# One hand-divided tile for w_down's blocks and their sums, with six block places in the 6-tile products

## The chip, the cores and the metric

One core of a Trainium2 chip runs the kernel. The metric is the device time of one execution in microseconds (us), as the median of several runs.

## The reference

One layer of a hybrid decoder in float32, on 512 tokens with 16 learned meta tokens ahead of them (D = 2048, feed-forward width 5632):

```python
n = rmsnorm(h, g_mix);  p = n @ w_in            # q, k, v | b, c, u
o = concat(rmsnorm(stick_breaking_attention(q, k, v)),      # 8 heads of 128
           rmsnorm(b * causal_dwconv3(c * u)))              # 1024 channels
h = h + o @ w_out
n2 = rmsnorm(h, g_ffn)
h = h + (silu(n2 @ w_gate) * (n2 @ w_up)) @ w_down
return h[:, N_META:]
```

The change lies in the preparation of the weights of the last two lines, the feed-forward part, and in the places that `w_out`'s tiles share with them.

## The kernel before

**Products.** A float32 product is made of three products of rounded halves: each operand is split into hi (a rounded copy) and lo (the rest), and TensorE adds hi·hi, hi·lo and lo·hi (L702, L703 and L704). Weights are the stationary operand, 128x128 at a time; 256 token columns stream past.

**Pairs.** Gate, up and down are computed by a scheme that does a 2x2 block product with 7 products instead of 8. A *pair* is one such set of four weight blocks, 11, 12, 21 and 22. There are 44 pairs of gate and up (8 k tiles a block, pairs 0 to 43), four pairs of `w_down` that hold two output columns of 4 k tiles each (pairs 44 to 47, results 512 wide), and 24 pairs of `w_down` with 6 k tiles (pairs 48 to 71, in three chunks of the feed-forward width). The seven products of a pair use, in this order, the weights 11, t1 = 11+12, t2 = t1+22, 22, t3 = 12+22, 21 and t2+21. They accumulate into three PSUM banks in the order x, z, x, z, x, y, x. `pair_product` drains them: ScalarE copies x, z, x after products 1, 2 and 3 (L727, L729, L731); VectorE reads z after product 4 (L733) and x after product 5 (L737), and y after product 6 (L740). Product 7 writes bank x again, and so it cannot begin before L737 has read it.

**Preparation of weights.** It runs two products ahead of TensorE (`S_AHEAD` = 2), in steps of `prepare_pair`. `load_quad` (L591) issues the DMA of one block on SyncE's queue (SP). `split_quad` makes hi on ScalarE (L609) and lo on VectorE (L610). `add_quads` makes t1 and t3 on VectorE (L616), L650 makes t2 in t1's buffer, and `add_last` (L623) adds 21 into t2. A block of the next pair is loaded as soon as the same block of this pair has been read for the last time: 11 after t1, 12 after t3, 22 after its split, 21 after it has been added into t2. `load_wide` (L601) fetches `w_out`'s tiles into the same buffers before pair 0.

**Buffers.** Pool `sw` has one buffer for each of the tags `b11`, `b12`, `b21` and `b22`, two for the tag `sum` (t1 and t3 take them in turn), and three for the tag `s` (hi and lo of a product): 48 KB of each partition. In pairs with 6 k tiles a quarter of each buffer is unused.

**Order.** The kernel is written in product order, and a scheduler orders each engine's queue by the dependences of the tiles; the preparation has high priority. Which instruction stands first on VectorE therefore depends on which buffer comes free first.

**Other queues.** `gate` turns products into activations, splits them (L187 and L188) and stores them to DRAM by GpSimd's queue (POOL, L894), the last ones by SP's (L896); `load_acts` brings them back into a ring of places on POOL's queue (L932). `down` adds the results of the first chunks into the output in DRAM (L961, POOL).

Of the kernel before, what the change touches and what calls it, by code (L numbers as in the profile page):

```python
# [9 lines left out]
F32 = mybir.dt.float32  # L10
F32R = mybir.dt.float32r
# [4 lines left out]
P = 128  # L16
# [6 lines left out]
KT = D // P  # L23
FT = FF // P
# [9 lines left out]
def hybrid_layer(ctx: ExitStack, tc: tile.TileContext, xT, w_in, w_out, w_gu, w_down, vecs, out):  # L34
# [12 lines left out]
    def open_pool(name, bufs=1, **kw):  # L47
        return tc.alloc_tile_pool(name=name, bufs=bufs, reuse_waits="tile", **kw)
# [509 lines left out]
    sw = open_pool("sw", side="right")  # L558
    acc_h = hpool.tile([P, SEQ], F32, name="acc_h")
    hpool.tile([P, 24], F32, name="pad_h")  # L560
    pairs = []
# [17 lines left out]
    quads, sums, split_w, used = {}, {}, [], [0]  # L579
    S_AHEAD = 2  # L580
    ORDER = ("21", "11", "12", "22")
    WIDE = 2 * KT - 2

    def load_quad(i, q):
        if i < len(pairs):
            n, srcs = pairs[i]
            quads[i, q] = sw.tile([P, 8 * P], F32, tag=f"b{q}", name=f"b{q}_{i}")[:, : n * P]
            src, dst = srcs[("11", "12", "21", "22").index(q)], quads[i, q]
            if len(src.shape) == 3:
                dst = dst.rearrange("p (t c) -> p t c", t=2)  # L590
            nc.sync.dma_start(dst, src)  # L591

    wide = []

    def load_wide():

        i = len(wide)
        q = ORDER[(i + 2) % 4]
        if i < WIDE:
            wide.append(sw.tile([P, 8 * P], F32, tag=f"b{q}", name=f"wide{i}"))  # L600
            nc.sync.dma_start(wide[i], w_out[OUT_TILES[1 + i // 2], i % 2])  # L601
        else:
            wide.append(None)
            load_quad(0, q)

    def split_quad(src, n):
        t = sw.tile([P, 2, 8 * P], F32R, tag="s", bufs=S_AHEAD + 1, name=f"s{len(split_w)}")
        hi, lo = (t[:, i, : n * P] for i in range(2))
        sc.copy(hi, src)  # L609
        ve.tensor_tensor(lo, src, hi.bitcast(F32), ALU.subtract)  # L610
        split_w.append((hi, lo))

    def add_quads(i, name, a, b):
        n = pairs[i][0]
        sums[name] = sw.tile([P, 8 * P], F32, tag="sum", bufs=2, name=f"{name}_{i}")[:, : n * P]
        ve.tensor_tensor(sums[name], a, b, ALU.add)  # L616

    def add_t3(i, b):
        add_quads(i, "t3", b["12"], b["22"])
        load_quad(i + 1, "12")  # L620

    def add_last(i, b):
        ve.tensor_tensor(sums["t2"], sums["t2"], b["21"], ALU.add)  # L623
        load_quad(i + 1, "21")


    FIRST_ORDER = (5, 0, 1, 2, 3, 4, 6)
# [1 line left out]
    def prepare_pair():  # L629
        if len(split_w) < WIDE:  # L630
            with tc.high_priority():
                split_quad(wide[len(split_w)], 8)
                load_wide()
            return
        i, s = divmod(len(split_w) - WIDE, 7)
        if i == len(pairs):
            return
        n = pairs[i][0]
        if i == 0:
            s = FIRST_ORDER[s]  # L640
        with tc.high_priority():
            b = {q: quads[i, q] for q in ("11", "12", "21", "22") if (i, q) in quads}
            if s == 0:
                split_quad(b["11"], n)
                add_quads(i, "t1", b["11"], b["12"])
                load_quad(i + 1, "11")
            elif s == 1:
                split_quad(sums["t1"], n)
                sums["t2"] = sums["t1"]
                ve.tensor_tensor(sums["t2"], sums["t2"], b["22"], ALU.add)  # L650
                if i:
                    add_t3(i, b)
            elif s == 2:
                split_quad(sums["t2"], n)
                if not i:
                    add_t3(i, b)
            elif s == 3:
                split_quad(b["22"], n)
                load_quad(i + 1, "22")
            elif s == 4:  # L660
                split_quad(sums["t3"], n)
            elif s == 5:
                split_quad(b["21"], n)
                if i:
                    add_last(i, b)
            else:
                if not i:
                    add_last(i, b)
                split_quad(sums["t2"], n)

    def prepare_ahead(n):
        while len(split_w) < min(WIDE + 7 * len(pairs), used[0] + n):
            prepare_pair()
# [96 lines left out]
    for _ in range(4):  # L770
        load_wide()
# [11 lines left out]
    for i, j in enumerate(OUT_TILES):  # L783
# [8 lines left out]
        half, k = divmod(j, 8)  # L792
# [285 lines left out]
```

## Time and profile before

| what | value |
| --- | --- |
| runs | 2084.57, 2085.06 and 2085.66 us; median 2085.06 |
| profiled execution | 2083.91 us, span on the chip 2082.2 us, mean granted clock 0.998 |
| TensorE busy (PE) | 2056.2 us, 99% of the span |
| VectorE busy (DVE) | 1627.0 us, 78% |
| ScalarE busy (ACT) | 1016.3 us, 49% |
| GpSimd busy (POOL) | 370.4 us, 18% |
| weight blocks of gate and up, issue to landing | 176 loads of 512 KB, median 3.7 us |
| blocks of `w_down`, two columns | 16 loads of 512 KB, median 7.6 us |
| blocks of `w_down`, 6 k tiles | 96 loads of 384 KB, median 3.7 us |
| activations back from DRAM (ring) | 42 loads of 768 KB, median 13.3 us |

The span is the time from the first to the last instruction on the core; the execution's own time is slightly longer. Busy shares are means over stages with different limits, so what counts is what TensorE waits for in each stage. In the rows, a number in brackets behind an instruction is the idle time of its engine before it and what ended it; `t<-b,b` is a sum of two blocks, `s<-b,s` or `s<-t,s` the lo half of a split, `b<-w_down` a load.

### The profile page before, as it was taken

What the parts mean: (1) busy time and instruction counts of PE and PEld (TensorE: products, weight loads), DVE (VectorE), ACT (ScalarE), POOL (GpSimd) and SP (SyncE); (2) the same over time, 40 slices, a digit from 0 to 9 for tenths busy, and PEclk for the clock granted to TensorE, in tenths of its full rate; (3) what the DMA queues carried; (4) which work ended last, traced back from release to release, by engine and by line L of the source; (5) the groups of instructions that cost most, each with busy time, mean ns of one, the idle gap of its engine ahead of it and who ended that gap; (6) DMA issues with size and microseconds to landing.
All of it is one profiled execution on the core that took longest, in us unless ns stands there. A gap on an engine that the chain in (4) does not pass through costs nothing.

```text
span 2082.2 us, 39144 instructions
## 1 busy us (share of the span) xinstructions
PE 2056.2 (99%) x16086; PEld 1982.1 (95%) x16086; DVE 1627.0 (78%) x2133; ACT 1016.3 (49%) x1522; POOL 370.4 (18%) x499
## 2 busy tenths in 40 slices
PE   8999999999999999999999999999999999999999
PEld 7899999999998888999999999999999999989999
DVE  6877777533336769999898898898988977878888
ACT  6666666322223434555555555555555544444443
POOL 0111111010103454111111011011111242121210
PEclk9999999999999999999999999999999999999999
DMA  5222222222225557546555464455455999697764
GB/s 186 72 72 77 77 82 72 82 97 94 93 101 167 185 179 239 158 137 195 166 149 170 149 177 153 148 172 167 135 175 158 279 340 339 149 323 171 209 149 110
DMA packets 144116, 330.41 MB, mean 159 GB/s; under 512 B 12400, under 2 KB 62064, under 8 KB 143936
## 3 DMA queue, kind: packets, MB, share of 16 engines
q1 hardware_dynamic: 67456, 212.50, 30.6%
q0 software_dynamic: 76480, 115.40, 21.6%
q8 instruction: 126, 2.06, 0.4%
q14 instruction: 54, 0.44, 0.1%
HBM read 260.74 MB, written 67.11 MB: 157 GB/s over the span
## 4 chain that ended last, share of the span: by engine, by line
PE 91%; DVE 4%; DMA 3%; ACT 1%; issue 1%; SPq 0%; POOL 0%; DVEq 0%; ACTq 0%; POOLq 0%
PE x L702 10%; PE x L704 10%; PE x L703 10%; PE z L702 5%; PE z L704 5%; PE z L703 5%; PE po L682 3%; PE po L683 3%; PE po L681 3%; PE y L704 3%; PE y L703 3%; PE y L702 3%; DMA b<-w_down 2%; PE pv L173 2%; PE pv L175 2%; PE pu L177 1%
## 5 line engine op out<-in xcount | busy, mean ns | idle before, releaser
L609 ACT CAST s<-t 128x1024 fp32r<-128x1024 f32 (+1 forms) x288 | 283.2, 983 | 373.7 <-PE z L704 164.1
L610 DVE TENSOR_TENSOR s<-t,s 128x1024 fp32r<-128x1024 f32 (+1 forms) x288 | 326.8, 1135 | 99.4 <-ACT s L609 97.4
L704 PE MATMUL x<-f,s 128*128 128x256 f32 x1408 | 387.4, 275 | 1.7 <-DVE s L610 1.7
L703 PE MATMUL x<-f,s 128*128 128x256 f32 x1408 | 387.5, 275 | 0.2 <-DVE f L188 0.2
L702 PE MATMUL x<-f,s 128*128 128x256 f32 x1408 | 387.4, 275 | 0.2 <-ACT f L187 0.2
L609 ACT CAST s<-b 128x1024 fp32r<-128x1024 f32 (+1 forms) x216 | 212.4, 983 | 156.6 <-PE x L704 138.0
L704 PEld LDWEIGHTS x<-f,s 128*128 128x128 f32 x1408 | 264.3, 188 | 1.9 <-DVE s L610 1.9
L702 PEld LDWEIGHTS x<-f,s 128*128 128x128 f32 x1408 | 264.3, 188 | 0.7 <-ACT f L187 0.4
L703 PEld LDWEIGHTS x<-f,s 128*128 128x128 f32 x1408 | 264.3, 188 | 0.5 <-DVE f L188 0.4
L610 DVE TENSOR_TENSOR s<-b,s 128x1024 fp32r<-128x1024 f32 (+1 forms) x216 | 246.5, 1141 | 2.4 <-ACT s L609 1.8
L142 DVE TENSOR_TENSOR wlo<-raw,whi 128x512 fp32r<-128x512 f32 (+1 forms) x198 | 139.3, 705 | 134.8 <-ACT whi L141 133.9
L894 POOL DMA_DIRECT2D fd<-s x147 | 103.7, 922 | 690.5 <-DVE s L188 674.0
L141 ACT CAST whi<-raw 128x512 fp32r<-128x512 f32 (+1 forms) x198 | 121.1, 614 | 192.0 <-PE pu L175 65.6
L702 PE MATMUL z<-f,s 128*128 128x256 f32 x704 | 193.8, 275 | 0.7 <-ACT sides L729 0.7
L703 PE MATMUL z<-f,s 128*128 128x256 f32 x704 | 193.8, 275 | 0.2 <-DVE f L188 0.2
L704 PE MATMUL z<-f,s 128*128 128x256 f32 x704 | 193.7, 275 | 0.0
L616 DVE TENSOR_TENSOR t<-b,b 128x1024 f32<-128x1024 f32 (+1 forms) x144 | 165.5, 1149 | 21.8 <-DMA b<-w_down 17.3
L702 PE MATMUL x<-ring,s 128*128 128x256 f32 x608 | 167.8, 276 | 8.8 <-DVE d L737 6.4
L704 PE MATMUL x<-ring,s 128*128 128x256 f32 x608 | 167.4, 275 | 0.5 <-DVE s L610 0.5
L703 PE MATMUL x<-ring,s 128*128 128x256 f32 x608 | 167.3, 275 | 0.0
L702 PEld LDWEIGHTS z<-f,s 128*128 128x128 f32 x704 | 132.2, 188 | 0.9 <-ACT sides L729 0.9
L703 PEld LDWEIGHTS z<-f,s 128*128 128x128 f32 x704 | 132.2, 188 | 0.4 <-DVE f L188 0.4
(349 smaller groups left out, 5588.0 us busy)
## 6 DMA issues: line engine op xcount, KB each, us to landing
b<-w_gu SPq DMA_DIRECT2D x176, 512.0 KB, 3.7
raw<-w_in SPq DMA_DIRECT2D x92, 512.0 KB, 3.2
fd<-s POOLq DMA_DIRECT2D x147, 256.0 KB, 5.3
b<-w_down SPq DMA_DIRECT2D x96, 384.0 KB, 3.7
ring<-fd POOLq DMA_DIRECT2D x42, 768.0 KB, 13.3
wide<-w_out SPq DMA_DIRECT2D x30, 512.0 KB, 3.3
out_T<-d POOLq DMA_DIRECT2D x54, 256.0 KB, 4.7
b<-w_down SPq DMA_DIRECT2D x16, 512.0 KB, 7.6
```

Of the source, the lines that this page charges most:

```text
L141: sc.copy(hi[:, :c], raw)
L142: ve.tensor_tensor(lo[:, :c], raw, hi[:, :c].bitcast(F32), ALU.subtract)
L609: sc.copy(hi, src)
L610: ve.tensor_tensor(lo, src, hi.bitcast(F32), ALU.subtract)
L616: ve.tensor_tensor(sums[name], a, b, ALU.add)
L681: pe.matmul(ps, hi[:, kk], ah, start=k == 0, stop=False)
L682: pe.matmul(ps, hi[:, kk], al, start=False, stop=False)
L683: pe.matmul(ps, lo[:, kk], ah, start=False, stop=k == 7)
L702: pe.matmul(p, hi[:, kk], act[:, 0, k], start=start and j == k == 0, stop=False, skip_group_check=skip)
L703: pe.matmul(p, hi[:, kk], act[:, 1, k], start=False, stop=False, skip_group_check=skip)
L704: pe.matmul(p, lo[:, kk], act[:, 0, k], start=False, stop=k == n - 1, skip_group_check=skip)
L894: gp.dma_start(fd[c][s][:, :, k], t[:, :, i])
```

## The change

The pool's tags are replaced by two tiles that are divided by hand and have the same size together. `sw_split` holds the three hi and lo places in turn. `sw_in` holds blocks and sums. With 8 k tiles it has six places: four for blocks, one each for t1 (in which t2 is made) and t3. With 6 k tiles it has eight: six that the blocks take in turn, one each for t1 and t3. From pair 48 on, `load_next` gives a freed place to the block that is six blocks further on: when 11 is free, 22 of the next pair is loaded; when 12 is free, 21 of the next pair; when 22 is free, 11 of the pair after the next; when 21 is free, 12 of that pair. Before pair 48 a freed block is followed by the same block of the next pair, as it was. Line numbers behind this part move: L591 becomes L604, L609 and L610 become L632 and L633, L616 becomes L639, L733 becomes L758, L737 becomes L762.

```diff
+    QUADS = ("11", "12", "22", "21")
+    SIX = FT + KT // 4
+    sw_in = sw.tile([P, 6 * 8 * P], F32, name="sw_in")
+    sw_split = sw.tile([P, 6 * 8 * P], F32R, name="sw_split")
+
+    def w_place(t, n, i):
+        return t[:, i * n * P : (i + 1) * n * P]
+
+    def quad_place(i, q):
+        m = QUADS.index(q)
+        return w_place(sw_in, pairs[i][0], m if i < SIX else (4 * (i - SIX) + m) % 6)
+
     def load_quad(i, q):
         if i < len(pairs):
             n, srcs = pairs[i]
-            quads[i, q] = sw.tile([P, 8 * P], F32, tag=f"b{q}", name=f"b{q}_{i}")[:, : n * P]
+            quads[i, q] = quad_place(i, q)
...
+    def load_next(i, q):
+
+        m = QUADS.index(q)
+        if i < SIX:
+            load_quad(i + 1, q)
+            if i + 1 == SIX and m == 3:
+                load_quad(SIX + 1, QUADS[0])
+        else:
+            load_quad(i + 1 + (m + 2) // 4, QUADS[(m + 2) % 4])
...
-            wide.append(sw.tile([P, 8 * P], F32, tag=f"b{q}", name=f"wide{i}"))
+            wide.append(quad_place(0, q))
...
     def split_quad(src, n):
-        t = sw.tile([P, 2, 8 * P], F32R, tag="s", bufs=S_AHEAD + 1, name=f"s{len(split_w)}")
-        hi, lo = (t[:, i, : n * P] for i in range(2))
+        k = len(split_w) % (S_AHEAD + 1) * 2
+        hi, lo = (w_place(sw_split, n, k + i) for i in range(2))
...
     def add_quads(i, name, a, b):
         n = pairs[i][0]
-        sums[name] = sw.tile([P, 8 * P], F32, tag="sum", bufs=2, name=f"{name}_{i}")[:, : n * P]
+        sums[name] = w_place(sw_in, n, (4 if n == 8 else 6) + (name == "t3"))
         ve.tensor_tensor(sums[name], a, b, ALU.add)
 
     def add_t3(i, b):
         add_quads(i, "t3", b["12"], b["22"])
-        load_quad(i + 1, "12")
+        load_next(i, "12")
 
     def add_last(i, b):
         ve.tensor_tensor(sums["t2"], sums["t2"], b["21"], ALU.add)
-        load_quad(i + 1, "21")
+        load_next(i, "21")
...
-                load_quad(i + 1, "11")
+                load_next(i, "11")
...
-                load_quad(i + 1, "22")
+                load_next(i, "22")
...
                 split_quad(sums["t2"], n)
+                if i + 1 == SIX:
+                    load_quad(SIX + 1, QUADS[1])
```

## The prediction

> **What bounds the kernel now.** I read the busy time by stretches first: the gate/up pairs (833 to 1626), the four pairs of `w_down` with two output columns (1626 to 1722), and the pairs with products of 6 k tiles, where the six places are (1722 to 2060).
>
> ```profile
> core 0: us, PE busy (x) PEld busy (x) DVE busy (x) ACT busy (x) POOL busy (x), PEclk, DMA share, GB/s
> 833.00:1626.00 793.00, 792.32 (x6991) 792.12 (x6990) 714.26 (x800) 416.81 (x542) 105.11 (x149) 1.00 0.53 160
> 1626.00:1722.00 96.00, 95.41 (x840) 95.03 (x839) 79.55 (x81) 48.57 (x59) 33.05 (x40) 1.00 1.11 330
> 1722.00:2060.00 338.00, 329.21 (x2892) 328.21 (x2891) 288.17 (x386) 152.09 (x230) 63.63 (x78) 1.00 0.80 216
> ```
>
> TensorE is the bound everywhere: it misses 0.7 us of 793, 0.6 of 96, and 8.8 of 338. The change issues the same matmuls, so it can gain only from the last row's 8.8 us, and it loses wherever it makes TensorE wait. The waits of PE in 1722 to 2060 say what the 8.8 are:
>
> ```profile
> PE x L702 <- DVE d L737: 6.4, 4, 2.5
> PE x L702 <- ACT s L609: 2.4, 2, 1.5
> ```
>
> Six waits, all at the start of a pair's seventh product. That product writes the PSUM bank `x` that L737 reads, so it waits for L737. What L737 waits for stands in the chain of waits and the timeline, for the longest of the six:
>
> ```profile
> 1832.52 8.18 DMA b<-w_down
> ```
>
> ```profile
> 1840.79 0.96 DVE L616 TENSOR_TENSOR t<-b,b 128x768 f32<-128x768 f32 x1 [3.27 <-DMA b<-w_down]
> 1841.67 0.42 DVE L737 SCALAR_TENSOR_TENSOR d<-x,sides 128x256 f32<-128x256 f32 x1
> ```
>
> ```profile
> 1842.23 0.36 PE L702 MATMUL x<-ring,s 128*128 128x256 f32 x1 [2.50 <-DVE d L737]
> ```
>
> The load is block 22 of the next pair, issued when 22 of this pair has been split, 8.18 us on its way. t3 = 12+22 stands in DVE's queue for it, L737 stands behind t3, and 0.14 us after L737's end (1842.09) the product starts. So a late block 22 costs TensorE time through DVE's order, not because TensorE needs that block yet.
>
> **What the change takes away.** From pair 48 on, the load of 22 of the next pair goes out when 11 of this pair has been split, not 22.
>
> ```profile
> 1824.48 0.95 DVE L610 TENSOR_TENSOR s<-b,s 128x768 fp32r<-128x768 f32 x1
> ...
> 1833.53 0.96 DVE L616 TENSOR_TENSOR t<-b,b 128x768 f32<-128x768 f32 x1
> ```
>
> ```profile
> DMA to landing us min/median/max: 3.0/6.1/8.5
> ```
>
> The first row is the split of 11 in the pair of that stall; the load can be issued at its end, 1825.43, instead of 1832.52. The last line is the time to landing of all weight loads issued from 1820 to 1880. Even with 8.5 us it lands at 1833.9, where the sum waited until 1840.79. The 8.8 us go, all of them as far as these rows show. With each stall's restart counted I would not go over 10.
>
> **What the change adds unsaid: the order of the two sums.** Before, t1 and t3 take turns in two buffers (tag `sum`). The next pair's t1 takes the buffer that t3 has just left, the next t3 that of t2 (t2 is summed into t1's buffer, and is read last). After, t1 has a place of its own for ever and t3 another. The next t1 cannot be written until the last split of t2 has read its place; the next t3 can, as soon as t3 has been split. So in the built program DVE's order turns, in nearly every pair from the first gate/up pair on: before s(t3), t1', s(21), L733, s(t2), t3', L737; after s(t3), **t3'**, s(21), L758 (the old L733), s(t2), **t1'**, L762 (the old L737), where s() is the subtraction of a split and ' is the next pair. t1' needs blocks 11 and 12, t3' needs 12 and 22. Block 22 is therefore wanted where 11 was, four places sooner, and outside the 6-tile pairs its load is issued at the same event as before. Queued behind the waiting t3' on DVE are s(21) and s(t2), which TensorE's products 6 and 7 need, and L762, on whose bank product 7 waits. PE's order is the same; SP's, ACT's and POOL's nearly (two ring loads on POOL's queue go ahead of an output accumulation).
>
> Gate/up, an even pair:
>
> ```profile
> 1216.05 0.33 SPq L591 DMA_DIRECT2D b<-w_gu  x1
> ```
>
> ```profile
> DMA to landing us min/median/max: 3.1/3.1/3.1
> ```
>
> ```profile
> 1218.16 1.22 DVE L616 TENSOR_TENSOR t<-b,b 128x1024 f32<-128x1024 f32 x1
> ...
> 1224.32 0.42 DVE L737 SCALAR_TENSOR_TENSOR u<-x,sides 128x256 f32<-128x256 f32 x1
> ...
> 1226.01 0.28 PE L702 MATMUL x<-f,s 128*128 128x256 f32 x1
> ```
>
> Block 22 lands at 1219.15; t3' moves to where t1' starts, 1218.16: a wait of 1.0 us. L737 ends at 1224.74 and, with 0.14, has 1.13 us before the product that needs it. So it costs 0, though only just; DVE's idle time in between is a further reserve. In odd pairs the 128x1280 split of the activations goes ahead of t3', and the block is there. Only the first pair is worse: its block 22 lands late.
>
> ```profile
> 821.33 1.43 DVE L616 TENSOR_TENSOR t<-b,b 128x1024 f32<-128x1024 f32 x1 [0.98 <-DMA b<-w_gu]
> ```
>
> There t1' (1.15, below) used to run ahead of that wait and now comes behind it: +1.2.
>
> The two-column pairs, where loads are slow. Pair 45, DVE and then the start of its seventh product:
>
> ```profile
> 1674.60 1.23 DVE L610 TENSOR_TENSOR s<-t,s 128x1024 fp32r<-128x1024 f32 x1 [1.05 <-ACT s L609]
> 1675.86 1.23 DVE L616 TENSOR_TENSOR t<-b,b 128x1024 f32<-128x1024 f32 x1
> 1677.27 1.22 DVE L610 TENSOR_TENSOR s<-b,s 128x1024 fp32r<-128x1024 f32 x1 [0.18 <-ACT s L609]
> 1678.97 0.69 DVE L733 SCALAR_TENSOR_TENSOR d_first<-z,d_first 128x512 f32<-128x512 f32 x1 [0.48 <-PE z L704]
> 1679.98 1.23 DVE L610 TENSOR_TENSOR s<-t,s 128x1024 fp32r<-128x1024 f32 x1 [0.33 <-ACT s L609]
> 1681.63 1.23 DVE L616 TENSOR_TENSOR t<-b,b 128x1024 f32<-128x1024 f32 x1 [0.42 <-DMA b<-w_down]
> 1682.78 0.68 DVE L737 SCALAR_TENSOR_TENSOR d_first<-x,d_first 128x512 f32<-128x512 f32 x1
> ```
>
> ```profile
> 1684.14 0.28 PE L702 MATMUL x<-first,s 128*128 128x256 f32 x1
> ```
>
> t3' waited for its block until 1681.63. Now everything from s(21) on stands behind that. From start to next start: sum 1.15 (1681.63 to 1682.78), split 1.22 (its duration), combination 0.68 (its duration 0.69, less the overlap), split 1.26 (1674.60 to 1675.86), sum 1.15, L762 0.68, and 0.14 to PE: 6.28. The product starts at 1681.63 + 6.28 = 1687.9 instead of 1684.14: **+3.8**. The other pairs by the same chain, from when their t3' has its block to when product 7 started:
>
> ```profile
> 1642.40 1.23 DVE L616 TENSOR_TENSOR t<-b,b 128x1024 f32<-128x1024 f32 x1 [0.38 <-DMA b<-w_down]
> ...
> 1644.89 0.28 PE L702 MATMUL x<-f,s 128*128 128x256 f32 x1
> ...
> 1662.27 1.23 DVE L616 TENSOR_TENSOR t<-b,b 128x1024 f32<-128x1024 f32 x1
> ...
> 1664.19 0.36 PE L702 MATMUL x<-first,s 128*128 128x256 f32 x1
> ...
> 1700.69 1.23 DVE L616 TENSOR_TENSOR t<-b,b 128x1024 f32<-128x1024 f32 x1 [0.45 <-DMA b<-w_down]
> ...
> 1703.18 0.28 PE L702 MATMUL x<-first,s 128*128 128x256 f32 x1
> ```
>
> Pair 43, the last of gate/up, has 256-wide combinations (0.42 each, so 0.5 less): 1642.40 + 5.8 - 1644.89 = **+3.3**. Pair 46: 1700.69 + 6.28 - 1703.18 = **+3.8**. Pair 44: there s(21) goes ahead of t3' (so 5.06 behind it), and 1662.27 + 5.06 - 1664.19 = +3.1 at most. But pair 43's stall shifts that pair's loads by 3.3, and POOL's queue has run out by then:
>
> ```profile
> L932 POOL DMA_DIRECT2D first<-fd x2: 703/716/730, 1645.4 to 1646.0; - x2
> ...
> DMA to landing us min/median/max: 14.1/14.7/15.4
> ```
>
> ```profile
> DMA to landing us min/median/max: 4.6/4.6/4.6
> ```
>
> POOL's last loads of that burst land by 1661.4; the second line is the weight load issued between 1660 and 1661, in that gap. The sum of 1662.27 waited for nothing, so the block was there by then; if its load starts 3.3 later but takes 4.6 us, not the 6.6 (below) to 8.2 (above) of loads beside POOL's, it lands 2 to 3.6 sooner after its issue, which is about the shift and about the price: pair 44 **0**, with 3.1 as the other end. Pair 47, whose next pair is the first with 6 tiles:
>
> ```profile
> 1711.77 0.33 SPq L591 DMA_DIRECT2D b<-w_down  x1
> ```
>
> ```profile
> DMA to landing us min/median/max: 6.6/6.6/6.6
> ```
>
> ```profile
> 1722.22 0.28 PE L702 MATMUL x<-first,s 128*128 128x256 f32 x1
> ```
>
> Landing 1718.4, then the chain with 768-wide sums (0.88 by 1840.79 to 1841.67, twice) and one 768-wide split ahead of L762 (0.87): 6.28 - 0.54 + 0.87 = 6.6; 1718.4 + 6.6 - 1722.22 = **+2.8**, from 0 if POOL's queue has run out here too.
>
> A rule of the Trainium skill bears on these loads: its page "DMA: Bandwidth & Descriptors", section "Queues, rings and completion order", says that each DMA engine takes turns, packet by packet, between the queue rows that have work, so a weight load beside POOL's transfers gets only its turns. The trace agrees: the load of 1711.77 took 6.6 us, those in the gap and in gate/up 4.6 and 3.1. By that rule alone a pair whose load falls into a gap would cost nothing, which is rival (a).
>
> The last thing added is 221 wait-only instructions on DVE (the lo subtraction now names its wait for PE too). Such waits exist already:
>
> ```profile
> L610 DVEq EVENT_SEMAPHORE  x2: 21/21/21, 1210.3 to 1229.4; - x2
> ```
>
> At 21 ns each they could come to 4.6 us if all were on the path. DVE is idle for 79 of the 793 us of gate/up while TensorE misses 0.7, so I take 0, and keep 1 for the range.
>
> **Sum.** 1.2 + 3.3 + 0 + 3.8 + 3.8 + 2.8 = 14.9 lost, 8.8 gained: +6.1. I take 0.5 off, for the load's time in pairs 45 to 47 as the stretched stage thins the traffic: **+5.6**. The rows come from the profiled execution, 2083.9 us (span 2082.2), which would become 2089.5; it lies 1.15 under the median of 2085.06, so on the median the forecast is **2090.7**. A measurement here can tell about 0.2% (4.2 us) from no change, so this is just over it.
>
> **The rivals.** (a) The loads come free, not slower: each stall delays the next pair's loads, while most of POOL's ring loads go out by its own queue, not by TensorE, so later weight loads may meet a queue that has run empty. Against it: that burst on POOL's queue was over 14 us deep, and a shift of some 4 us a pair doesn't use that up at once. It decides from 3 us off each landing (6.6 or 8.2 to 4.6). Then pairs 44 and 47 cost 0 and 45 and 46 some 0.8 each: 1.2 + 3.3 + 1.6 - 8.8 = -2.7, 2082.4; with pair 43 free too, -6, 2079. Chance 0.25. (b) Gate/up pairs stall as well: 1.0 us of wait stands against 1.13 of slack there, and DVE is at 90%. At 0.5 us in each of 22 even pairs it is +11 on top: 2101. For it speaks the thin margin, against it the idle time of DVE behind the wait. Chance 0.07. (c) The early block 22 of the 6-tile pairs is second of two loads on SP's queue and lands 8.5 us on, at 1833.9, 0.4 late for its sum. If ring loads stretch it by 2 us more, some stalls stay: half of 8.8 gives 2095. Chance 0.13. (d) The order stays t1' first on the chip and only the gain comes: 2076. The built program speaks against it; 0.04.
>
> **How the numbers follow.** My case has 0.51. Its own range is 2087 (pair 47 free) to 2094 (pair 44 pays 3.1). Range for 8 in 10: from 2081.5, which takes in most of (a), to 2096, which takes in (c). Faster (under 2080.9): (d) and a part of (a), 0.13. Same (to 2089.2): the rest of (a) and a third of my case, 0.27. Slower: 0.60.
>
> **What would show it.** In the profile after, DVE's sum behind the split of t3 must read the blocks that block 22's load fills, and the waits of PE from 1722 on must be near 0 instead of 8.8. From 1640 to 1730 PE should show new waits of 3 to 4 us on DVE, with DVE waiting for `w_down`'s DMA ahead of s(21), in pairs 43, 45, 46 and 47; part of one may stand as a wait for s(21) in product 6. The gate/up row should still miss under 1 us. The forecast is wrong if the stage's weight loads take 4 us instead of 7, if gate/up loses more than 2 us, or if stalls stay in the 6-tile pairs.

## The result, and the profile after

The changed kernel takes 2090.65 us (median of 20 runs, 2088.55 to 2093.03); the kernel before took 2084.49 us in the same comparison (20 runs). The ratio is 1.0029, 95% interval 1.0022 to 1.0036: slower by 6.2 us, where +5.6 was forecast. The profiled execution after has a span of 2089.5 us, 7.3 more than before.

Here is the busy time by the same three stretches, with the borders moved along with the pairs:

```profile
core 0: us, PE busy (x) PEld busy (x) DVE busy (x) ACT busy (x) POOL busy (x), PEclk, DMA share, GB/s
833.00:1629.00 796.00, 795.05 (x7011) 794.69 (x7011) 712.93 (x800) 418.20 (x546) 105.16 (x149) 1.00 0.55 159
1629.00:1737.00 108.00, 99.26 (x845) 97.95 (x844) 77.36 (x80) 48.49 (x59) 32.22 (x38) 0.98 1.06 311
1737.00:2067.00 330.00, 328.51 (x2897) 328.31 (x2896) 291.55 (x389) 152.62 (x230) 64.45 (x78) 1.00 0.83 217
```

TensorE now misses 8.7 us in the two-column pairs, where it missed 0.6, and 1.5 in the last stretch, where it missed 8.8. That 1.5 is the last wait of pair 47, which falls just behind the border: from 1745 on the view of PE's waits is empty. The view of PE's waits from 1600 to 1740 names them (L727, L728 and L729 are the old L702, L703 and L704; the fourth line, 0.5 us in pair 44, stood there before too):

```profile
PE y L729 <- DVE sw_split L633: 7.0, 4, 2.0
PE x L727 <- DVE d_first L762: 1.5, 1, 1.5
PE x L727 <- DVE d L762: 0.9, 1, 0.9
PE x L729 <- DVE sw_split L633: 0.5, 1, 0.5
PE x L727 <- DVE u L762: 0.3, 1, 0.3
```

The first line is new in kind: product 6 (bank `y`, weights 21) waits for the lo half of block 21. Its split stands behind the waiting t3' on VectorE. PE's timeline gives each wait its place (in brackets the idle time):

```profile
1649.16 0.39 PE L729 MATMUL y<-f,sw_split 128*128 128x256 f32 x1 [1.97 <-DVE sw_split L633]
...
1652.32 0.36 PE L727 MATMUL x<-f,sw_split 128*128 128x256 f32 x1 [0.34 <-DVE u L762]
...
1690.79 0.38 PE L729 MATMUL y<-first,sw_split 128*128 128x256 f32 x1 [1.81 <-DVE sw_split L633]
...
1713.55 0.39 PE L729 MATMUL y<-first,sw_split 128*128 128x256 f32 x1 [1.80 <-DVE sw_split L633]
...
1717.24 0.36 PE L727 MATMUL x<-first,sw_split 128*128 128x256 f32 x1 [0.89 <-DVE d L762]
...
1735.52 0.39 PE L729 MATMUL y<-first,sw_split 128*128 128x256 f32 x1 [1.46 <-DVE sw_split L633]
...
1739.81 0.35 PE L727 MATMUL x<-first,sw_split 128*128 128x256 f32 x1 [1.49 <-DVE d_first L762]
```

These are pairs 43, 45, 46 and 47; in each the split of 21 and then L762 come late, and pair 44 has no new wait. The chain behind pair 45's wait, from the chain of waits, and VectorE's timeline beside it:

```profile
1680.74 7.54 DMA sw_in<-w_down
```

```profile
1688.37 1.23 DVE L639 TENSOR_TENSOR sw_in<-sw_in 128x1024 f32<-128x1024 f32 x1 [5.49 <-DMA sw_in<-w_down]
1689.51 1.22 DVE L633 TENSOR_TENSOR sw_split<-sw_in,sw_split 128x1024 fp32r<-128x1024 f32 x1
1690.64 0.69 DVE L758 SCALAR_TENSOR_TENSOR d_first<-z,d_first 128x512 f32<-128x512 f32 x1
1691.24 1.22 DVE L633 TENSOR_TENSOR sw_split<-sw_in,sw_split 128x1024 fp32r<-128x1024 f32 x1
1692.50 1.23 DVE L639 TENSOR_TENSOR sw_in<-sw_in 128x1024 f32<-128x1024 f32 x1
1693.64 0.68 DVE L762 SCALAR_TENSOR_TENSOR d_first<-x,d_first 128x512 f32<-128x512 f32 x1
```

VectorE stands idle for 5.49 us with t3' (L639) at its head, and then works off what queued up behind it: split of 21, L758, split of t2, t1', L762. That is the order read from the built program, and the chain from 1688.37 to L762's end is 5.95 us long. Before, this t3' came last but one in the row, and waited 0.42 us for its block.

### The profile page after: what moved, and what is told of

Its sections match the earlier page's. It is cut to its first block, busy times and chain, and to the rows that moved or that the text cites. A ratio compares the mean times of both kernels' runs of the same rounds, so it can differ in the third digit from the quotient of the medians.

```text
span 2089.5 us, 39364 instructions
## 1 busy us (share of the span) xinstructions
PE 2060.1 (99%) x16086; PEld 1985.5 (95%) x16086; DVE 1623.7 (78%) x2133; ACT 1015.9 (49%) x1522; POOL 368.5 (18%) x499
## 4 chain that ended last, share of the span: by engine, by line
PE 92%; DVE 3%; DMA 2%; issue 1%; ACT 1%; SPq 0%; POOL 0%; DVEq 0%; ACTq 0%; POOLq 0%
PE x L727 11%; PE x L729 11%; PE x L728 10%; PE z L727 5%; PE z L729 5%; PE z L728 5%; PE y L729 3%; PE y L728 3%; PE y L727 3%; PE po L706 3%; PE po L708 3%; PE po L707 3%; DVE sw_split L633 2%; PE pv L173 2%; PE pv L175 1%; PE pu L177 1%
## 5 line engine op out<-in xcount | busy, mean ns | idle before, releaser
L632 ACT CAST sw_split<-sw_in 128x1024 fp32r<-128x1024 f32 (+1 forms) x534 | 526.3, 987 | 570.1 <-PE z L728 164.7
L633 DVE TENSOR_TENSOR sw_split<-sw_in,sw_split 128x1024 fp32r<-128x1024 f32 (+1 forms) x534 | 614.8, 1152 | 80.3 <-ACT sw_split L632 77.9
L729 PE MATMUL x<-f,sw_split 128*128 128x256 f32 x1408 | 388.4, 276 | 4.4 <-DVE sw_split L633 4.4
L728 PE MATMUL x<-f,sw_split 128*128 128x256 f32 x1408 | 388.4, 276 | 1.5 <-DMA f<-fx 1.3
L727 PE MATMUL x<-f,sw_split 128*128 128x256 f32 x1408 | 388.8, 276 | 0.9 <-DVE u L762 0.7
L729 PEld LDWEIGHTS x<-f,sw_split 128*128 128x128 f32 x1408 | 265.4, 188 | 4.6 <-DVE sw_split L633 4.6
L728 PEld LDWEIGHTS x<-f,sw_split 128*128 128x128 f32 x1408 | 265.3, 188 | 1.9 <-DMA f<-fx 1.5
L727 PEld LDWEIGHTS x<-f,sw_split 128*128 128x128 f32 x1408 | 265.4, 189 | 1.7 <-issue 1.1
L639 DVE TENSOR_TENSOR sw_in<-sw_in 128x1024 f32<-128x1024 f32 (+1 forms) x144 | 165.0, 1147 | 57.9 <-issue 33.1
L727 PE MATMUL z<-f,sw_split 128*128 128x256 f32 x704 | 193.8, 275 | 0.6 <-ACT sides L754 0.6
L728 PE MATMUL z<-f,sw_split 128*128 128x256 f32 x704 | 193.7, 275 | 0.2 <-DVE f L188 0.2
L729 PE MATMUL z<-f,sw_split 128*128 128x256 f32 x704 | 193.6, 275 | 0.0
L729 PE MATMUL x<-ring,sw_split 128*128 128x256 f32 x608 | 167.3, 275 | 0.5 <-DVE sw_split L633 0.5
L727 PE MATMUL x<-ring,sw_split 128*128 128x256 f32 x608 | 167.3, 275 | 0.0
L728 PE MATMUL x<-ring,sw_split 128*128 128x256 f32 x608 | 167.2, 275 | 0.0
L727 PEld LDWEIGHTS z<-f,sw_split 128*128 128x128 f32 x704 | 132.2, 188 | 0.8 <-ACT sides L754 0.8
L728 PEld LDWEIGHTS z<-f,sw_split 128*128 128x128 f32 x704 | 132.2, 188 | 0.4 <-DVE f L188 0.4
L729 PEld LDWEIGHTS z<-f,sw_split 128*128 128x128 f32 x704 | 132.2, 188 | 0.0
L729 PEld LDWEIGHTS x<-ring,sw_split 128*128 128x128 f32 x608 | 114.1, 188 | 0.7 <-DVE sw_split L633 0.7
```

Source lines behind the costliest of these rows:

```text
L727: pe.matmul(p, hi[:, kk], act[:, 0, k], start=start and j == k == 0, stop=False, skip_group_check=skip)
L728: pe.matmul(p, hi[:, kk], act[:, 1, k], start=False, stop=False, skip_group_check=skip)
L729: pe.matmul(p, lo[:, kk], act[:, 0, k], start=False, stop=k == n - 1, skip_group_check=skip)
```

## The experiments

Each was timed against the kernel before in runs on the same chip; differences in us are against that.

**1. The order alone undone.** In the changed kernel t1 and t3 swap their places from pair to pair, so that the next t1 again takes what t3 left. The places, the early loads and the additional waits stay.

```diff
-        sums[name] = w_place(sw_in, n, (4 if n == 8 else 6) + (name == "t3"))
+        sums[name] = w_place(sw_in, n, (4 if n == 8 else 6) + ((name == "t3") ^ (i % 2 == 0)))
```

> The changed kernel with t1 and t3 taking turns in their two places from pair to pair, in all pairs, so that VectorE's order is again the one of before (next t1 ahead, next t3 last), while the six places and the early loads stay. Theory (the order of the sums costs, the early loads gain): the waits of TensorE from 1640 to 1740 us (11.5 us in the profile after) and the 2.7 us more in the first pair go, the 8.8 to 10 us saved in the 6-tile pairs stay: 2075 us, 9 to 10 under before. Rival W (the hand-divided tile costs, by its 221 more waits or by dependences on a shared tile): stays at 2088 to 2091. Rival C (earlier loads crowd the queues): somewhere from 2080 to 2086, with waits left in the two-column pairs.

Measured: 2072.99 us against 2084.55, ratio 0.995 (0.9937 to 0.9962). Here are its stretches:

```profile
833.00:1629.00 796.00, 795.43 (x7018) 795.23 (x7017) 717.57 (x803) 418.01 (x544) 105.14 (x149) 1.00 0.55 160
1629.00:1725.00 96.00, 95.64 (x843) 95.44 (x843) 80.19 (x82) 48.34 (x59) 34.50 (x40) 1.00 1.11 332
1725.00:2060.00 335.00, 335.00 (x2958) 335.00 (x2958) 296.96 (x396) 156.58 (x236) 63.84 (x78) 1.00 0.82 218
```

TensorE misses nothing at all in the 6-tile pairs and 0.4 us in the two-column pairs, at the same DMA share of 1.11 as before. So the early loads gain all that they can, and the loss lies in the order of the two sums. This version beats both kernels. One part of the expectation failed: in the first pair the product still waited 3.0 us (4.4 in the changed kernel, 1.7 before); the account of that pair below says why.

**2. The old order in the 6-tile pairs alone.** The same edit, with `(i % 2 == 0 and n == 6)`.

> Turns only in the 6-tile pairs (from the sums of pair 48 on); gate/up and two-column pairs keep the changed order. Theory: only pair 47 gains, whose next sums are the first with 6 tiles: its 1.6 + 1.65 us go, so some 3 under the changed kernel, 2087 to 2088; the 6-tile pairs have no waits with either order. If the order in the 6-tile pairs mattered it would be lower than that. Rival W: 2090.7, unchanged.

Measured: 2087.55 us against 2084.55, ratio 1.0013 (1.0004 to 1.0021). The waits of pairs 43, 45 and 46 are nearly as in the changed kernel, those of pair 47 are gone. In the 6-tile pairs there is no wait with either order.

**3. The old order in gate/up and two-column pairs alone.** The same edit, with `(i % 2 == 0 and n == 8)`.

> Turns only in gate/up and the two-column pairs; the 6-tile pairs keep the changed order. Theory: all of the loss goes except pair 47's 3 us: 2078. Rival W: 2088 to 2091. Rival C: 2083 to 2089.

Measured: 2077.16 us against 2084.55, ratio 0.9967 (0.9955 to 0.9979). What is left in PE's timeline is pair 47, with the price it had in the changed kernel on its second wait and less on its first:

```profile
1721.78 0.39 PE L729 MATMUL y<-first,sw_split 128*128 128x256 f32 x1 [0.60 <-DVE sw_split L633]
...
1726.07 0.35 PE L727 MATMUL x<-first,sw_split 128*128 128x256 f32 x1 [1.48 <-DVE d_first L762]
```

**4. The tile alone.** Experiment 1's kernel with a fixed place for each block, and the loads of before.

```diff
-        return w_place(sw_in, pairs[i][0], m if i < SIX else (4 * (i - SIX) + m) % 6)
+        return w_place(sw_in, pairs[i][0], m)
...
     def load_next(i, q):
...
+        load_quad(i + 1, q)
```

> The hand-divided tiles with turns in all pairs and the loads of before: each block has a fixed place and is followed by the same block of the next pair in the 6-tile pairs too. What is left of the change is the tile and its additional waits on VectorE. Theory: the time of before, 2084.5 to 2085, with the six waits of 8.8 us in the 6-tile pairs. Rival W: 2088 to 2091 (221 waits of 21 ns on the path would be 4.6 us).

Measured: 2084.19 us against 2084.55, ratio 1.0002 (0.9993 to 1.001). The tile and its waits cost nothing that can be measured (the interval reaches from 1.5 us less to 2 us more), and without the early loads the waits of the 6-tile pairs are back (PE's waits from 1745 on; L720 and L755 of this kernel are L727 and L762 of the changed one):

```profile
PE x L720 <- DVE d L755: 6.3, 5, 2.2
PE x L720 <- ACT sw_split L627: 1.5, 1, 1.5
PE y L722 <- DVE sw_split L628: 0.2, 1, 0.2
```

**5. The order alone, in the kernel before.** Two tags instead of one; no tile, no early loads.

```diff
-        sums[name] = sw.tile([P, 8 * P], F32, tag="sum", bufs=2, name=f"{name}_{i}")[:, : n * P]
+        sums[name] = sw.tile([P, 8 * P], F32, tag=f"sum{name}", name=f"{name}_{i}")[:, : n * P]
```

> The kernel before with one edit: t1 and t3 have a buffer each (two tags) and no longer take turns. No hand-divided tile, no six places, loads as before. Theory: the order of the sums turns as in the change, so the same waits appear in the first pair and in pairs 43 to 47 (some 14 us), and in the 6-tile pairs, whose block 22 is still issued late, they grow: next t3 is wanted some 7 us sooner, a load beside the ring loads takes 6.1 us, one without them 3.0; in about half of 24 pairs 2 to 4 us each. In all 25 to 50 over before: 2110 to 2135. Rival W (the tile costs, not the order): the time of before, 2085.

Measured: 2128.68 us against 2086.58, ratio 1.0207 (1.0185 to 1.0229). The two-column pairs lose as much as in the changed kernel: added up over the starts of all matmuls from 1640 to 1745, beyond the usual 0.113 us from one to the next, 14.2 us here, 14.5 in the changed kernel and 1.5 before. In the 6-tile pairs PE's waits (from 1745 on) come to

```profile
PE x L702 <- DVE d L737: 17.2, 11, 4.7
PE x L702 <- issue: 4.1, 3, 3.0
PE y L704 <- DVE s L610: 1.7, 1, 1.7
```

and VectorE's own wait for the block, in the view of its waits over the same stretch, is

```profile
DVE t L616 <- DMA b<-w_down: 36.9, 21, 5.3
```

So the order makes the late block dear wherever loads are slow, and the early loads of the 6-tile pairs are what keeps the changed kernel from this there.

**6. Block 22 by half.** The changed kernel, with half of block 22 loaded in the two-column pairs.

```diff
                 dst = dst.rearrange("p (t c) -> p t c", t=2)
+                if q == "22":
+                    dst, src = dst[:, :1], src[:, :1]
```

> The changed kernel, but block 22 of the two-column pairs 44 to 47 is loaded by half (256 KB, its first output column; the other half keeps old data, which leaves out part of the weights). The order of VectorE stays. Theory (the price is the landing of block 22 by the chain behind next t3): 384 KB take 6.1 us beside the ring loads and 512 KB 7.4, so 256 KB some 4.8: landing 2.6 us sooner takes the waits of pairs 43, 45 and 46 (2.6 + 2.0 + 3.0 us) to near 0 and leaves pair 47 (its next block 22 is one of 6 tiles): 2083 to 2084.5. Rival (the order itself makes VectorE's chain too long, whenever the block lands): 2089 to 2091, the waits as they are.

Measured: 2087.66 us against 2086.58, ratio 1.0005 (0.9996 to 1.0014). By that ratio it is 1 us over before, 5 under the changed kernel, but not the 7 expected. The halved loads that pairs 43, 45 and 46 wait for took 5.8 to 5.9 us instead of 7.2 to 7.7, so 1.4 to 1.9 less and not 2.6. And the edit moved one more thing: in pair 44 the scheduler now put t3' ahead of the split of the activations and of 21, and that pair, free in the changed kernel, now cost 1.9 and 1.0 us ahead of products 6 and 7. The costs of pairs 43, 45 and 46 did fall, by 1.4 to 2.2 us, but with the order moved as well this run alone does not show why, and the next one leaves the order as it is. In VectorE's timeline (lines stand two further down here: L641 is L639, L635 is L633):

```profile
1664.33 1.23 DVE L641 TENSOR_TENSOR sw_in<-sw_in 128x1024 f32<-128x1024 f32 x1 [3.33 <-DMA sw_in<-w_down]
1665.47 1.48 DVE L188 TENSOR_TENSOR s<-odd,s 128x1280 fp32r<-128x1280 f32 x1
1666.88 1.22 DVE L635 TENSOR_TENSOR sw_split<-sw_in,sw_split 128x1024 fp32r<-128x1024 f32 x1
```

**7. The same for pairs 46 and 47 only**, where VectorE's order stays exactly that of the changed kernel.

```diff
+                if q == "22" and i > 45:
+                    dst, src = dst[:, :1], src[:, :1]
```

> The changed kernel, with block 22 loaded by half (256 KB instead of 512) only for pairs 46 and 47; the other half keeps old data, which leaves out part of the weights. VectorE's order is that of the changed kernel in every pair. Halving saved 1.4 to 1.9 us from issue to landing where it was tried before. Theory (the price is the landing of block 22 by the chain behind next t3): pair 45 waits 1.7 to 1.9 us less and pair 46 too, pairs 43, 44 and 47 as they were; 3.5 to 5 us under the changed kernel with the slow clock after pair 45's wait, if that goes: about 2086 to 2087. Rival (the order alone makes the chain too long): pairs 45 and 46 wait as they did, 2090 to 2091.

Measured: 2087.04 us against 2084.17, ratio 1.0009 (1.0 to 1.0019); by that ratio it is some 4 us under the changed kernel. The two loads landed in 6.2 and 6.0 us instead of 7.5 and 7.7. Pair 46's cost, by the starts of the matmuls, fell from 3.3 to 2.0 us, by 1.3 for a landing 1.7 sooner. Pair 45's split into two short ones,

```profile
1688.19 0.39 PE L731 MATMUL y<-first,sw_split 128*128 128x256 f32 x1 [0.43 <-DVE sw_split L635]
...
1691.88 0.35 PE L729 MATMUL x<-first,sw_split 128*128 128x256 f32 x1 [0.88 <-DVE d_first L764]
```

and what it cost fell from 3.7 to 1.9 (in the changed kernel a slow clock, told of below, is part of it). The price follows the landing of block 22, not the order by itself: with the block early, in the 6-tile pairs, neither order makes TensorE wait (experiments 1 and 2). The Trainium skill, page "DMA: Bandwidth & Descriptors", section "Queues, rings and completion order", has each DMA engine take turns between queues by packets; by that rule a load of half the bytes needs half the turns. The trace fits the direction, but only 1.3 of 7.5 and 1.7 of 7.7 us went with half of the bytes.

## Why the prediction was right

The direction, the size and the mechanism came out as forecast: the 6-tile pairs' waits went, and the order of the sums cost more elsewhere. Experiments 1, 4 and 5 show the parts one by one: order alone +42 (without early loads), tile alone 0, early loads with the old order -11.6. The terms below come from one profiled execution of each kernel: they say by how much the matmuls fall further behind those of the kernel before, start against start, in each place.

| term | forecast | measured |
| --- | --- | --- |
| ahead of the first pair | 0 | -0.8 |
| first pair | +1.2 | +4.7 |
| gate/up | 0 | +0.8 |
| pair 43 | +3.3 | +2.9 |
| pair 44 | 0 | -0.4 |
| pair 45 | +3.8 | +3.7 |
| pair 46 | +3.8 | +3.3 |
| pair 47 | +2.8 | +3.5 |
| 6-tile pairs | -8.8 | -10.4 |

That the sum came within 0.6 us of the measured 6.2 is partly luck: the first pair lost 3.5 us more than forecast, and the 6-tile pairs gained 1.6 more.

**6-tile pairs.** Forecast by PE's recorded idle time; by starts each wait cost some 0.26 us more, as the matmul that waited and the one behind it start late by more than the idle time.

**First pair.** The term that was furthest off, though not for the order of the sums. From the landing of block 22 to the product that waited for the chain behind it, 3.8 us passed before and 5.3 in the changed kernel: +1.5, where +1.2 was forecast. The experiments bear it out: 4.0 us where the order is the old one (1, 3, 4), 5.2 to 6.4 where it is the new one (2, 5, 6, 7). Two things were not in the forecast. Block 22's load took 7.9 us to land instead of 6.6; it took 8.0 to 8.2 in experiments 1, 3, 4, 6 and 7, with either order, 7.2 in experiment 5 and 6.3 in experiment 2, and why stays open. And the product that waited, with those behind it, ran at a slow clock, which cost 2.1 us (below); all seven experiments have such a stretch here, of 1.1 to 2.0 us, and the profile before has none. In VectorE's timeline and PE's:

```profile
821.81 2.95 DVE L639 TENSOR_TENSOR sw_in<-sw_in 128x1024 f32<-128x1024 f32 x2 [3.05 <-DMA sw_in<-w_gu]
824.68 2.29 DVE L633 TENSOR_TENSOR sw_split<-sw_in,sw_split 128x1024 fp32r<-128x1024 f32 x1
...
827.02 0.58 PE L729 MATMUL x<-f,sw_split 128*128 128x256 f32 x1 [4.37 <-DVE sw_split L633]
```

**Gate/up.** The margin of 0.13 us held nearly everywhere; one wait of 0.4 us at 1420.93 appeared. At the same place experiments 2, 5 and 6 have one of 0.3 us or less, experiment 7 has none, and neither has any kernel with the old order. Rival (b) came to 0.8 us, not 11.

**Pair 44 and rival (a).** The relief came where it was forecast and hardly elsewhere. The times to landing of the block that pair 44 waits for and of the one that pair 47 waits for were

```profile
DMA to landing us min/median/max: 4.8/4.8/4.8
```

```profile
DMA to landing us min/median/max: 6.9/6.9/6.9
```

Before, pair 44's took 7.6. The blocks that pairs 43, 45 and 46 wait for had 7.2, 7.5 and 7.7 us, 0.1 to 0.4 less than in the profile before, and pair 47's 0.3 more. That is all there was of rival (a); for pairs 45 to 47, where 0.5 us was taken off for thinner traffic, it comes to 0.3.

**Pairs 43, 45, 46.** The chain was taken 0.2 us long: I charged the full duration of the split of 21 and of the first combination, whose followers start 1.13 and 0.60 us after them. The shorter loads took off 0.1 to 0.4 more. Part of pair 45's cost is slow clock in place of its second wait (below).

**Additional waits.** Experiment 4 puts the 0 to 4.6 us at 0, within 2 us. Rivals (c) and (d) did not come: after pair 47 the changed kernel has no wait of TensorE, and the order did turn.

## What to carry to other kernels

When rotating buffers become fixed places, look at which instruction each place holds back: a scheduler such as this one orders an engine's queue by what is free first, and a fixed place can pull a step that needs a late block ahead of steps that need none. Here one expression, letting two sums change places from pair to pair, turned a loss of 6 us into a gain of 11.6. Gains by an earlier load and losses by a changed order are best read apart, pair by pair, from the engine that stands at the head of the chain.

## What the runs showed of the hardware that was not expected

A wait of about 2 us can halve TensorE's clock for a while. After pair 45's wait of 1.81 us the matmuls started 0.21 us apart instead of 0.113, for 16 matmuls in a row, from 1692.27 on. The windows before, in and after it (the eighth column is the granted clock):

```profile
1690.79:1692.00 1.21, 1.21 (x10) 1.21 (x11) 1.21 (x2) 0.00 (x0) 0.00 (x0) 1.00 1.23 409
1692.00:1695.40 3.40, 3.40 (x18) 3.40 (x18) 3.37 (x5) 0.71 (x1) 0.77 (x1) 0.51 1.22 395
1695.60:1699.00 3.40, 3.40 (x32) 3.40 (x31) 2.81 (x3) 1.19 (x3) 2.15 (x4) 1.00 1.12 389
```

Half the clock for 3.4 us spread these matmuls by 1.6 us. Here little of that was a loss of its own, as it took the place of the second wait that the neighbours show: L762 ended at 1694.32, and product 7 began at 1694.62. In experiment 5, where pair 45 kept the full clock, it cost 3.5 us against 3.7 here. The waits of 1.97 and 1.80 us in pairs 43 and 46 had no such aftermath; the first pair's 4.4 us had one of 2.1 us, and in experiment 5 five of them after 1745 spread the matmuls by 9.0 us. The Trainium skill, page "TensorE: Matmul & The Clock Gate", section "Part 1: The HAM clock gate", says that TensorE's clock is halved after an idle window of some 3.4 us, in windows that run free of the program. The halving and the 3.4 us agree; that it needs 3.4 us of idling does not agree with 1.81 us here.

The traces' record of the granted clock shows the windows. In every trace the clock changes only whole multiples of 3.41 us apart (in the changed kernel at 825.08 and 1692.06, for instance), wherever the waits lie. Cut into such windows, the nine profiles have 17 from 815 us to the last products in which TensorE had the full clock and, by the profile, idled for 1.77 us or more in all: the clock was halved at the end of 16 of them (the other, in experiment 5, held 1.80). It was halved after none with 1.68 us or less. Pair 45's wait lies whole in one window, while borders cut those of pairs 43 and 46, whose larger parts are 1.47 and 1.01 us. So, as far as these runs show, it takes idling for about half of a window, and where the borders fall decides whether a wait of 2 us is hit.
